# A state-space and attention layer: the pacing of background products beside attention goes from 62.5 to 57.5 of 64

## Chip, cores and metric

One NeuronCore of one Trainium2 chip runs the whole layer. The metric is device time in microseconds (us) of one execution, as the median of three runs. Times in the rows below are us from the start of the profiled span. Engines: PE is TensorE, PEld its weight loads, DVE is VectorE, ACT is ScalarE, POOL is GpSimd, and SP issues the transfers (DMA).

## What is computed

The reference is a decoder layer on x (2048 tokens by 1024 channels, float32). In short:

```python
u    = layer_norm(x) * (1 + scale) + shift
x_ssm, z_ssm, q, k, v, f, z_attn, g_ssm, g_attn = split(u @ w_in)
a, b = split(gelu(s5(x_ssm)) @ w_glu)
y1   = (a * sigmoid(b) * silu(z_ssm)) @ w_proj_ssm
y2   = (forgetting_attention(q, k, v, f) * silu(z_attn)) @ w_proj_attn
out  = layer_norm(alpha * x + ((sigmoid(g_ssm) * y1 + sigmoid(g_attn) * y2) @ w_out) * gate)
```

Attention has 8 heads of 64 channels, is causal, and subtracts a running forgetting bias from the scores.

## The kernel before

**Stages.** Up to about 1010 us the kernel normalizes x, projects it, and runs the state-space scan. Then comes attention, with the products of w_glu and w_proj_ssm beside it (to 1619.5 us). The merge products (w_proj_attn), the output projection (w_out) and the last layer norm close the program. Every float32 product is split into a high and a low part and made of three matmuls.

**Rounds of attention.** One round handles a pair of query blocks (256 queries) of a head: 64 rounds, 8 to a head, numbered 0 to 63 (`rounds`, in `hybrid_layer`). In round p of a head there are 256*(p+1) keys, so the first rounds of a head are short and the last are long. `scores` issues score matmuls (`sc<-ks,qd`), and DVE subtracts the bias and takes maxima (`srow<-sc,fb`). `exponentials` runs on ACT (`srow<-srow,nm`), and DVE writes the reciprocal of the sum (`lb`). `weights_times_v` transposes on PE (`pt<-ident,srow`). Then ACT and DVE copy the result in two parts (`ph`, `pl`), and PE multiplies them by v (`acc<-ph,vs`, `acc<-pl,vs`). The first thing PE writes with a round's `lb` is `acc<-ident,lb`, one per round: it serves below as the mark of a round. `normalize` closes a round on POOL and stores it (`oz_sc<-oo`).

**Products beside it.** `background` has 64 such products: 32 of w_glu and 32 of w_proj_ssm. One product is `mm4`: 12 matmuls into one bank (`bg<-bh,wh`, `bg<-bl,wh`, `bg<-bh,wl`), 512 columns each. Of the last 32, each takes a place of a ring of three (`zt`): SP loads a gate into it (`zt<-gs_sc`), DVE combines it with the product (`zt<-zt,bg`, 128x512), and SP stores the result (`ms_sc<-zt`). After them `background` makes the 64 merge products (12 matmuls of 256 columns each, in banks `bg` and `pt`), which also take places of `zt` (`zt<-ga_sc` and `zt<-ms_sc` fill the halves). ACT and POOL split a result (`mh`, `ml`) for the output projection (`pp<-woh,mh` and so on).

**What sets the order.** The order on every engine is fixed when the program is built. `Model` keeps a rough clock, and `merge` emits from the first stream, in order of rank, whose next step would not wait. `exponentials`, `weights_times_v`, `normalize` and `scores` rank first; then `finish`, `tail`, `inputs`, `weight_chunks` and `background`; `output`, which loads w_out (`wor<-in_w_out_dram`) and splits it (`woh` on ACT, `wol` on DVE and POOL), comes after them. A merge product also waits for `"fin" in done`, and `output` sets that after attention has ended. So `output` is emitted when `background` cannot go on.

**The pacing.** `share(r)` tells how many products must have been emitted before the scores of round r may be, in proportion to the keys up to there:

```python
return AHEAD * (36 * h + p_ * (p_ + 1) / 2) / (36 * NH) - 3
...
yield until(lambda: ck["jobs"] >= share(r))
```

Where the attention streams would wait, `background` is emitted whether or not the share is reached.

Of the kernel before, what the change touches and what calls it, by code (L numbers as in the profile page):

```python
# [16 lines left out]
S = 2048  # L17
D = 1024
NW = 4          # token windows of 512
WT = 512  # L20
KD = D // 128
NG = 32         # state-space groups
GH = 16         # channels of a group
CL = 8          # tokens of a chunk
NCH = S // CL   # chunks
CW = WT // CL   # chunks of a window
NH = 8
# [9 lines left out]
PKN = 163       # of a group: Bbar 16 | swapped 16 | C 16 | swapped 16 | tables 64 | powers 19 | A^7..A^0 16  # L37
# [4 lines left out]
class Model:  # L42
    """A rough clock of the engines, by which the order of emission is chosen (it computes no data)."""

    # from the end of an instruction to the start, on another engine (or the same), of one that needs it
# [34 lines left out]
    def deps(self, e, kw):  # L80
        """When the operands are there for engine e (whose own accesses are in order)."""
        rd, wt = self.aps(kw)
        r = 0.0
        for n in rd:
            if n in self.wr:
                end, by = self.wr[n]
                r = max(r, end + self.lat(e, by))
            for h in self.held:
                if n in h[2]:           # (a transfer that is still to come)
                    r = max(r, max(h[0] + 1100, self.t["sp"] + 1100, self.t["dma"]) + 1700)  # L90
# [43 lines left out]
    def run(self, e, op, kw):  # L134
# [11 lines left out]
        for n in wt:  # L146
            # parts of a tile that transfers fill do not wait for each other
            self.ac.setdefault(n, {})["in" if e == "sp" else e] = end
            self.wr[n] = (end, e)

    def settle(self, rd, wt, dma=False):
        """Emit what is held and has to come before a read of rd and a write of wt (transfers may fill parts of a
        tile in any order)."""
# [14 lines left out]
    def merge(self, streams):  # L168
        """Emit from the first stream whose next step would not wait; streams come in order of rank."""
# [27 lines left out]
class Engine:  # L197
    """An engine whose instructions the model sees."""
# [14 lines left out]
    def when(self, **kw):  # L213
        """When an instruction with these operands could start."""
# [3 lines left out]
    def soon(self, op, /, **kw):  # L218
        """A stream's step: the instruction, emitted once it would not wait."""
# [3 lines left out]
    def later(self, op, /, **kw):  # L223
        """The instruction, emitted once its operands are there (the streams go on meanwhile)."""
# [6 lines left out]
def hybrid_layer(ctx: ExitStack, tc: tile.TileContext, x, c, w_ada, b_ada, w_in, b_f, lam_re, lam_im,  # L231
# [32 lines left out]
    def pround(o, i):  # L264
        """Pool's copy into float32r (its rounding)."""
# [19 lines left out]
    # maskb[q, k] = 0 where k <= q, NEG elsewhere  # L285
# [4 lines left out]
    # ------------------------------------------------------------------ phase 1: input projection  # L290
    esl = ExitStack()               # left: until the projection is done
# [11 lines left out]
    def ps_tile(n=[0]):  # L303
        """One of four banks, which attention later has for scores (three) and outputs."""
# [7 lines left out]
    def bg_tile(n=None):  # L312
        if n is not None and n % 4 > 1:         # (the banks of the transposes, once attention is done)
            return pt_tile()
# [5 lines left out]
    def bank():  # L320
        """Whichever of the two banks of bg_tile is free."""
# [12 lines left out]
    def split_wide(raw, n):  # L334
        """A stream that splits a chunk of weights; the tiles are there at once."""
# [8 lines left out]
    def rstd_of(p, mv, n):  # L344
        """1 / sqrt(var + eps) of the variances mv[:, :, 1]."""
# [21 lines left out]
    def until(f):  # L367
        """A condition to wait on, whatever the time."""
        return lambda: 0.0 if f() else None

    def modulation():
        """shift | 1 + scale of silu(c) @ w_ada + b_ada, as columns, 128 channels at a time."""
# [3 lines left out]
        act.activation(out=one, in_=ident[:, 0:1], func=AF.Sqrt)    # (its table is there when the layer norm needs it)  # L376
# [43 lines left out]
    def early_keys():  # L420
        """Two column tiles of the keys' weights, with which the first window goes on while the next one comes."""
# [7 lines left out]
    def modulation_columns():  # L429
        """Sums over the partitions, as columns."""  # L430
# [17 lines left out]
    def column_sums(acc, n, c0):  # L448
        """mods[:, c0:] = sums of acc over its partitions, as columns, + b_ada."""
# [34 lines left out]
    def normalized():  # L484
        """Windows of tokens, less their mean and over their spread."""
# [21 lines left out]
    def modulated():  # L507
        """u = normalized * (1 + scale) + shift, channels on partitions."""
# [28 lines left out]
    def low_parts():  # L537
        """The two parts of u."""
# [23 lines left out]
    def products_of(ps, w, hi, lo, c0):  # L562
        """A tile of columns of the projection of a window."""
# [7 lines left out]
    def store_parts(kind, m, w, ps):  # L571
        """Queries (scaled) or keys, in two parts."""
# [92 lines left out]
    # the other columns, with the state-space branch alongside  # L665
# [55 lines left out]
    def forget_bias():  # L721
        """f_sc[h, t] = cumulative log_sigmoid(f + b_f)."""
        with ExitStack() as es:
# [10 lines left out]
            # log1p(e) = 2 artanh(s), s = e / (2 + e) <= 1/3  # L734
# [25 lines left out]
    def gate():  # L760
        """The gate part of the modulation, as a row (scaled by 1/16, which the merge leaves)."""
# [17 lines left out]
    def ssm_params():  # L779
        """Per group: input and output matrices, powers and phases, written to pk_sc."""  # L780
        with ExitStack() as es:
            p0 = pl(es, "spp", side="right")
            pk = p0.tile([128, NG, PKN], F32, name="pk")
            uv = p0.tile([128, 4, NG], F32, name="uv")    # phase of A^8 (cos, sin), zoh (re, im)
# [22 lines left out]
            # cosine and sine of arg = n pi/2 + r  # L807
# [21 lines left out]
            od, ev = t32(), t32()       # quadrant: odd * sign, even * sign  # L829
# [7 lines left out]
            def lin(o, p0_, q0, p1, q1, sub):  # L837
                """o = p0 q0 +- p1 q1"""
# [10 lines left out]
            # 0..8: real A^k, both halves; 9..17: imaginary A^k, [-; +]; 18: |A|^8; 19, 20: phase of A^8  # L849
# [941 lines left out]
```

## Time and profile before

| what | value |
|---|---|
| runs, device time | 1916.01, 1917.60, 1920.11 us (median 1917.6) |
| span of the profiled execution, first to last instruction | 1913.3 us |
| median less span (launch and end) | 4.3 us |
| PE busy | 1833.8 us (96%) |
| DVE, ACT, POOL busy | 1082.5 (57%), 775.1 (41%), 923.6 us (48%) |
| attention with its products | about 1012 to 1619.5 us |
| last product to first output matmul | 1623.6 to 1656.7 us |

For the profiled execution the span is what is given of its own time; the runs are timed without the profiler. PE is busy nearly all the time, so the places to look at are those where it is not, and those where its granted clock is below 1.00.

### The profile page before, as it was taken

How to read it: one execution, taken by the hardware profiler on the slowest of the kernel's cores; microseconds unless marked ns; L12 is line 12 of the kernel's file. 1: busy time of each engine (PE TensorE's matmuls, PEld its weight loads, DVE VectorE, ACT ScalarE, POOL GpSimd, SP SyncE). 2: the span in 40 equal slices, each digit the busy share in tenths (PEclk: the TensorE clock that was granted, in tenths of full speed). 3: DMA queues.
4: the chain of work that ended last, by engine and by line, in shares of the span. 5: the costliest groups of instructions: out<-in, count | busy, mean ns of one | idle time of the engine just before them, and what ended most of it. 6: DMA issues, size and time to landing. Idle time of an engine off the chain costs nothing. (4 is left out here: it accounts for less than half of the span.)

```text
span 1913.3 us, 30538 instructions
## 1 busy us (share of the span) xinstructions
PE 1833.8 (96%) x10104; PEld 1565.5 (82%) x10104; DVE 1082.5 (57%) x2886; ACT 775.1 (41%) x1849; POOL 923.6 (48%) x1343
## 2 busy tenths in 40 slices
PE   4999999998999999999998999999999999899997
PEld 3789988886787888888887888988889888788886
DVE  8651114734555555552004777876777866567666
ACT  5441111121433444443114767876767866311110
POOL 5222111113889999995306566376543436533110
PEclk9899999998999999999998999999999999999999
DMA  9434346654333333335217365265364543744432
GB/s 302 138 86 119 94 110 183 149 133 121 101 94 105 100 105 97 105 101 138 91 50 189 98 169 140 77 183 152 113 201 131 151 137 127 260 146 136 131 123 89
DMA packets 276915, 252.37 MB, mean 132 GB/s; under 512 B 66396, under 2 KB 211828, under 8 KB 276756
## 3 DMA queue, kind: packets, MB, share of 16 engines
q1 hardware_dynamic: 276756, 250.41, 45.7%
q8 instruction: 80, 1.31, 0.3%
q14 instruction: 79, 0.65, 0.1%
HBM read 159.50 MB, written 86.63 MB: 129 GB/s over the span
## 5 line engine op out<-in xcount | busy, mean ns | idle before, releaser
L209 PE MATMUL pp<-uh,hi 128*128 128x512 f32 x1136 | 451.0, 397 | 0.0
L209 PE MATMUL pp<-uh,lo 128*128 128x512 f32 x1136 | 446.0, 393 | 0.0
L209 PE MATMUL pp<-ul,hi 128*128 128x512 f32 x1136 | 445.1, 392 | 0.0
L209 ACT ACTIVATE st<-pp 128x512 f32<-128x512 f32 (+2 forms) x168 | 93.9, 559 | 439.1 <-PE pp L209 383.4
L209 DVE TENSOR_TENSOR pl<-pt,ph 128x512 fp32r<-128x512 f32 (+1 forms) x288 | 183.3, 657 | 122.3 <-ACT ph L209 121.7
L209 PEld LDWEIGHTS pp<-uh,lo 128*128 128x128 f32 x1136 | 214.2, 189 | 46.3
L209 PEld LDWEIGHTS pp<-uh,hi 128*128 128x128 f32 x1136 | 216.4, 190 | 41.5
L209 PEld LDWEIGHTS pp<-ul,hi 128*128 128x128 f32 x1136 | 214.7, 189 | 41.9
L209 ACT ACTIVATE srow<-srow,nm 128x512 f32<-128x512 f32 (+2 forms) x320 | 207.6, 653 | 0.4 <-DVE nm L209 0.3
L209 ACT ACTIVATE ph<-pt 128x512 fp32r<-128x512 f32 (+1 forms) x288 | 159.8, 572 | 64.4 <-PE pt L209 51.6
L209 DVE CUSTOM_DVE_ANT_0 srow<-sc,fb 128x512 f32<-128x512 f32 (+3 forms) x288 | 163.0, 594 | 21.9 <-PE sc L209 21.9
L209 PE MATMUL sc<-ks,qd 128*128 128x512 f32 (+2 forms) x640 | 163.7, 381 | 7.1 <-DMA qd<-q_sc 7.1
L209 PE MATMUL pt<-ident,srow 128*128 128x128 f32 x1088 | 159.3, 275 | 8.7 <-DVE pl L209 4.7
L209 PE MATMUL acc<-ph,vs 128*128 128x256 f32 x576 | 163.0, 308 | 2.5 <-POOL ph L209 2.5
L209 POOL TENSOR_TENSOR oo<-oo 64x256 f32<-64x256 f32 x128 | 93.7, 732 | 143.0 <-ACT oo L209 140.0
L209 POOL TENSOR_SCALAR hi<-raw 128x512 fp32r<-128x512 f32 x60 | 39.9, 665 | 237.8 <-PE pp L209 191.7
L209 PEld LDWEIGHTS pt<-ident,srow 128*128 128x128 f32 x1088 | 128.4, 141 | 27.2 <-DVE pl L209 9.5
L209 PE MATMUL acc<-pl,vs 128*128 128x256 f32 x576 | 147.4, 282 | 0.5 <-DVE pl L209 0.5
L209 PE MATMUL bg<-bh,wh 128*128 128x512 f32 (+1 forms) x384 | 140.2, 365 | 5.1 <-DVE zt L209 5.1
L209 PE MATMUL bg<-bh,wl 128*128 128x512 f32 (+1 forms) x384 | 138.1, 360 | 0.0
L209 PE MATMUL bg<-bl,wh 128*128 128x512 f32 (+1 forms) x384 | 137.8, 359 | 0.0
L209 PEld LDWEIGHTS sc<-ks,qd 128*128 128x128 f32 x640 | 107.9, 193 | 24.4 <-issue 8.4
(240 smaller groups left out, 3811.3 us busy)
## 6 DMA issues: line engine op xcount, KB each, us to landing
xt<-in_x_dram SPq DMA_DIRECT2D x32, 512.0 KB, 3.7
qd<-q_sc SPq DMA_DIRECT2D x64, 256.0 KB, 5.4
raw<-in_w_in_dram SPq DMA_DIRECT2D x30, 512.0 KB, 4.5
wada<-in_w_ada_dram SPq DMA_DIRECT2D x16, 512.0 KB, 7.0
k_sc<-st SPq DMA_DIRECT2D x32, 256.0 KB, 3.3
v_sc<-st SPq DMA_DIRECT2D x32, 256.0 KB, 2.3
q_sc<-st SPq DMA_DIRECT2D x16, 512.0 KB, 3.3
gs_sc<-st SPq DMA_DIRECT2D x32, 256.0 KB, 2.3
```

The lines of the kernel that those rows point to most:

```text
L209: return fn(kw["out"], 0.0) if op == "memset" else fn(**kw)
```

## The change

One number: `AHEAD`, the products that the pacing asks for by the end of attention.

```diff
-    AHEAD = 62.5    # products beside attention, of 64, that it has by its end
+    AHEAD = 57.5
```

(The diff also drops comments.) No instruction is added or removed: PE has 10042 matmuls and transposes both ways, 768 of them with 512 columns for the 64 products. What moves is the order. The first 6025 of PE's instructions keep it (to round 21). Of the 768 matmuls, 750 stood ahead of the last `acc<-pl,vs` of round 63 before, and 714 stand there now: 36 matmuls, or three products, have moved behind it. From round 55 to that last matmul PE's order is the same as before.

PE, rounds 35 to 36 (behind the mark of round 35), before:

```order
L209 MATMUL sc<-ks,qd 128x512 x6
L209 MATMUL bg<-bh,wh 128x512
L209 MATMUL bg<-bl,wh 128x512
L209 MATMUL bg<-bh,wl 128x512
L209 MATMUL acc<-ph,vs 128x256
L209 MATMUL acc<-pl,vs 128x256
L209 MATMUL acc<-ph,vs 128x256
L209 MATMUL acc<-pl,vs 128x256
L209 MATMUL bg<-bh,wh 128x512
L209 MATMUL bg<-bl,wh 128x512
L209 MATMUL bg<-bh,wl 128x512
```

and now, from the same score matmuls to the mark of round 36:

```order
L209 MATMUL sc<-ks,qd 128x512 x6
L209 MATMUL acc<-ph,vs 128x256
L209 MATMUL acc<-pl,vs 128x256
L209 MATMUL acc<-ph,vs 128x256
L209 MATMUL acc<-pl,vs 128x256
...
L209 MATMUL pt<-ident,srow 128x128 x8
L209 MATMUL sc<-ks,qd 128x512 x6
L209 MATMUL pt<-ident,srow 128x128 x4
L209 MATMUL sc<-ks,qd 128x256 x2
L209 MATMUL sc<-ks,qd 128x512 x2
L209 MATMUL acc<-ident,lb 128x128
```

Before, 12 product matmuls stood between the marks of rounds 35 and 36; now none does, and four more score matmuls do. Over rounds 35 and 36 together it is 24 before and 9 now, with six more score matmuls; over rounds 27 and 28 it is 15 and 3, with four more.

SP, from the last gate load of the 64 products to the loads of w_out, before:

```order
L209 DMA ms_sc<-zt 128x512
L209 DMA zt<-gs_sc 128x512
L209 DMA ms_sc<-zt 128x512
L209 DMA zt<-ga_sc 128x256
L209 DMA zt<-ms_sc 128x256
L209 DMA ms_sc<-zt 128x512
L209 DMA zt<-ga_sc 128x256
L209 DMA zt<-ms_sc 128x256
L209 DMA oz_sc<-oo 64x256
L209 DMA wor<-in_w_out_dram 128x1024 x3
L209 DMA ms_sc<-zt 128x512
```

and now:

```order
L209 DMA ms_sc<-zt 128x512
L209 DMA zt<-gs_sc 128x512
L209 DMA wraw<-in_w_proj_attn_dram 128x4x128
L209 DMA ms_sc<-zt 128x512
L209 DMA zt<-ga_sc 128x256
L209 DMA zt<-ms_sc 128x256
L209 DMA ms_sc<-zt 128x512
L209 DMA zt<-ga_sc 128x256
L209 DMA zt<-ms_sc 128x256
L209 DMA wor<-in_w_out_dram 128x1024 x3
L209 DMA ms_sc<-zt 128x512
```

The store of the last round (`oz_sc<-oo`) moved ahead by a few issues. The loads of w_out keep their place: behind the store of the last product but one, and ahead of the store of the last.

DVE, behind the second merge product, before:

```order
L209 TENSOR_TENSOR wol_18474<-wor,woh_18472 128x512 x3
L209 SCALAR_TENSOR_TENSOR zt<-zt,pt 128x256
L209 TENSOR_TENSOR zt<-zt 128x256
L209 SCALAR_TENSOR_TENSOR zt<-zt,pt 128x256
L209 TENSOR_TENSOR zt<-zt 128x256
L209 SCALAR_TENSOR_TENSOR zt<-zt,bg 128x256
L209 TENSOR_TENSOR zt<-zt 128x256
L209 TENSOR_TENSOR wol_18474<-wor,woh_18472 128x512 x2
```

and now:

```order
L209 TENSOR_TENSOR wol_18474<-wor,woh_18472 128x512 x2
L209 SCALAR_TENSOR_TENSOR zt<-zt,pt 128x256
L209 TENSOR_TENSOR wol_18474<-wor,woh_18472 128x512
L209 TENSOR_TENSOR zt<-zt 128x256
L209 SCALAR_TENSOR_TENSOR zt<-zt,pt 128x256
L209 TENSOR_TENSOR zt<-zt 128x256
L209 TENSOR_TENSOR wol_18474<-wor,woh_18472 128x512
L209 SCALAR_TENSOR_TENSOR zt<-zt,bg 128x256
```

The third piece of w_out moved one step back, the fourth moved ahead of the fifth merge product. On PE three output matmuls (`pp`) now stand ahead of the 13th merge product and six more ahead of the 14th; before, all 14 came ahead of the first output matmul.

## Rows read from the trace of the kernel before

**Rows 1.** Windows by stage; columns: us, busy us (x instructions) per engine, PEclk, DMA share, GB/s.

```profile
1217.50:1534.80 317.30, 310.40 (x1999) 273.74 (x1998) 244.00 (x793) 231.55 (x586) 162.94 (x261) 0.99 0.50 146
1623.60:1656.70 33.10, 24.16 (x169) 23.29 (x169) 18.99 (x31) 13.15 (x26) 25.02 (x25) 0.90 0.85 277
1656.70:1903.60 246.90, 246.90 (x1370) 215.72 (x1368) 165.95 (x350) 26.24 (x71) 59.61 (x72) 1.00 0.41 132
```

**Rows 2.** Timeline of PE: first product matmul behind attention, first merge product, one at low clock, the ninth.

```profile
1619.53 0.39 PE L209 MATMUL bg<-bh,wh 128*128 128x512 f32 x1
...
1623.64 0.28 PE L209 MATMUL bg<-bh,wh 128*128 128x256 f32 x1
...
1637.09 0.41 PE L209 MATMUL pt<-bh,wh 128*128 128x256 f32 x1
...
1640.75 0.28 PE L209 MATMUL bg<-bh,wh 128*128 128x256 f32 x1
```

**Rows 3.** Timeline of PE: matmuls with idle time before them, in brackets with the releaser.

```profile
1334.83 0.30 PE L209 MATMUL acc<-ident,lb 128*128 128x128 f32 x1 [1.45 <-DVE lb L209]
...
1352.73 0.30 PE L209 MATMUL acc<-ident,lb 128*128 128x128 f32 x1 [0.97 <-DVE lb L209]
...
1636.28 0.58 PE L209 MATMUL pt<-bh,wh 128*128 128x256 f32 x1 [3.86 <-DVE zt L209]
...
1646.13 0.39 PE L209 MATMUL bg<-bh,wh 128*128 128x256 f32 x1 [3.79 <-DVE zt L209]
...
1653.18 0.39 PE L209 MATMUL bg<-bh,wh 128*128 128x256 f32 x1 [0.97 <-DVE zt L209]
...
1655.19 0.39 PE L209 MATMUL bg<-bh,wh 128*128 128x256 f32 x1 [0.32 <-DVE zt L209]
```

**Rows 4.** Windows from round mark to round mark: rounds 27, 28, 33, 34, 35, 36.

```profile
1269.65:1276.79 7.14, 7.14 (x50) 6.43 (x49) 6.44 (x25) 4.44 (x11) 3.34 (x7) 1.00 0.36 100
1276.79:1286.66 9.87, 9.87 (x67) 8.53 (x66) 8.92 (x30) 7.81 (x21) 9.55 (x13) 1.00 0.68 205
...
1326.51:1334.83 8.32, 5.87 (x36) 4.74 (x35) 4.42 (x16) 4.69 (x14) 4.40 (x9) 1.00 0.88 234
1334.83:1342.39 7.56, 7.56 (x40) 6.82 (x41) 5.96 (x23) 4.51 (x11) 5.06 (x7) 0.77 0.53 154
1342.39:1352.73 10.34, 9.37 (x58) 7.97 (x57) 8.62 (x27) 8.07 (x23) 10.05 (x14) 1.00 0.45 123
1352.73:1361.94 9.21, 9.21 (x62) 8.32 (x63) 8.95 (x29) 6.32 (x15) 4.67 (x8) 1.00 0.63 192
```

**Rows 5.** The page's costliest groups: DVE's operation on a score tile.

```profile
L209 DVE CUSTOM_DVE_ANT_0 srow<-sc,fb 128x512 f32<-128x512 f32 (+3 forms) x288 | 163.0, 594 | 21.9 <-PE sc L209 21.9
```

**Rows 6.** Timeline of SP's queue behind attention.

```profile
1621.48 0.32 SPq L209 DMA_DIRECT2D zt<-ga_sc  x1
...
1622.38 0.38 SPq L209 DMA_DIRECT2D ms_sc<-zt  x1
1625.13 0.32 SPq L209 DMA_DIRECT2D zt<-ga_sc  x1
...
1626.02 0.47 SPq L209 DMA_DIRECT2D oz_sc<-oo  x1
1626.58 1.50 SPq L209 DMA_DIRECT2D wor<-in_w_out_dram  x3
```

**Rows 7.** Timeline of DVE behind attention.

```profile
1623.84 0.69 DVE L209 SCALAR_TENSOR_TENSOR zt<-zt,bg 128x512 f32<-128x512 f32 x1 [2.03 <-PE bg L209]
...
1634.67 1.22 DVE L209 TENSOR_TENSOR wol<-wor,woh 128x512 fp32r<-128x512 f32 x1 [0.46 <-ACT woh L209]
1635.82 0.41 DVE L209 SCALAR_TENSOR_TENSOR zt<-zt,pt 128x256 f32<-128x256 f32 x1
...
1638.38 0.41 DVE L209 SCALAR_TENSOR_TENSOR zt<-zt,bg 128x256 f32<-128x256 f32 x1
...
1640.98 0.69 DVE L209 TENSOR_TENSOR wol<-wor,woh 128x512 fp32r<-128x512 f32 x1 [1.11 <-ACT woh L209]
```

## The prediction

> **What bounds the kernel now.** I first read the windows by stage, to see where PE is not full. In the output projection it is: 246.90 of 246.90 us busy at a granted clock of 1.00 [rows 1]. In the stretch of attention in which the order changes (rounds 21 to 54) it is busy 310.40 of 317.30 us, so 6.9 us are idle. Between the last of the 64 products and the first output matmul it is busy only 24.16 of 33.10 us, at a granted clock of 0.90 [rows 1]. So attention is close to PE-bound, and the hole behind it is the worst place: 8.94 us idle, and about (1 - 0.90) x 33.1 = 3.3 us of clock.
>
> Next I looked at each gap. The hole has four: 3.86, 3.79, 0.97 and 0.32 us, 8.94 in all, and each ends with DVE's work on a `zt` tile [rows 3]: a merge product cannot start because its bank has not been emptied. A matmul of 256 columns lasts 0.41 us behind the first gap against 0.28 before it [rows 2], the half clock of 1.2 GHz. In attention the idle time is made of gaps of about 1 us, and the two shown end with DVE's `lb` [rows 3]: there the softmax chain was late.
>
> Last, I read DVE and SP in the hole. DVE's operation for the third merge product starts at 1635.82, behind a `wol` that waited for ACT [rows 7], and that in turn for w_out. The loads of w_out start at 1626.58 [rows 6], 2.9 us after the last product ended on PE at 1623.64 [rows 2].
>
> **The change, part by part.** PE's work is the same; 36 matmuls move. From 1619.53 to 1623.64 PE made 18 of them [rows 2]: 4.11 / 18 = 0.228 us each, so 36 take 8.2 us.
>
> 1. *Attention, rounds 21 to 54: -8.2 us*, if PE stays as full as it was.
> 2. *Behind attention: +8.2 us.* The three products run there back to back, at full clock. What they issue must keep pace: a load into `zt`, 0.69 us on DVE [rows 7] and a store. The store at 1622.38 let the next load of that place go at 1625.13 [rows 6], so it took 2.75 us. Taking a load of as many bytes at the same, a place is held about 6.2 us, and three places give a product every 2.1 us; PE needs 12 x 0.228 = 2.7 us. So SP's extra pairs of transfers and DVE's operations are hidden, by some 0.6 us a product; without that cover PE would wait for them.
> 3. *DVE in the thinned rounds: +1.4 us.* Rounds 35 and 36 lose 15 product matmuls and gain six score matmuls, that is three tiles. PE was busy 9.37 + 9.21 = 18.58 us there [rows 4]; it now needs 18.58 - 15 x 0.228 + 6 x 0.228 = 16.5 us (score matmuls taken at the price of others with up to 512 columns). DVE was busy 8.62 + 8.95 = 17.57 us [rows 4]. With three more tiles of 0.594 us [rows 5] and one combination of 0.69 us less it needs 18.7 us, 2.2 more than PE. Rounds 27 and 28 lose 15 - 3 = 12 and gain four. PE: 17.01 - 2.7 + 0.9 = 15.2 us. DVE: 6.44 + 8.92 + 1.2 - 0.69 = 15.9 us, 0.7 more. Upper end: 2.9 us, if DVE is filled without a gap and PE waits for all of it. Lower end: nothing, if the neighbouring rounds take up DVE's lag; three score banks and three `ph`/`pl` pairs let it lag a little. I take the middle, since round 35 shows the wait already (0.97 us on `lb`) and rounds 27 and 28 show none [rows 3, 4].
> 4. *The hole: no gain from more cover.* This is the choice on which the forecast rests. One would expect three more products, 8.2 us of PE, to hide the loads of w_out. But the order puts these loads in SP's queue behind the store of the last product but one, before and now alike, and that store comes only when PE has made that product. So w_out still starts about 2.5 to 3 us after the last product, however many products ran before it, and the three that moved pass ahead of it. The store of the last round now stands earlier in SP's queue, which takes one issue of 0.47 us [rows 6] out of the way. I count nothing for that.
> 5. *DVE's order in the hole: 0.* The third merge product no longer waits for the third `wol`: its operation could start at 1634.67 in place of 1635.82 [rows 7], -1.15 us. But the fifth, at 1638.38, now stands behind the `wol` that ran at 1640.98 for 0.69 us [rows 7]. That would let the ninth product, which takes its bank, start at about 1641.9 in place of 1640.75 [rows 2], +1.1 us. I take the middle of the two.
> 6. *Output matmuls ahead of the 13th and 14th merge products: -1.3 us.* Nine of them (9 x 0.228 = 2.1 us) stand where PE idled 0.97 and 0.32 us [rows 3]. Lower bound of this gain: nothing, if their own pieces of w_out are late.
>
> Sum: -8.2 + 8.2 + 1.4 + 0 + 0 - 1.3 = +0.1 us on a span of 1913.3, so 1913.4. The median of the runs lies 4.3 us above this span and I carry that over: **1917.7 us**. The launch, the projection, the scan, rounds 0 to 20 and the last layer norm keep their times.
>
> **The rivals.**
>
> *Filled hole (faster).* The hole goes: 8.94 us of gaps and 3.3 us of clock, with item 3 kept: 1917.6 + 1.4 - 12.2 = 1906.8 us. For it: the gaps are real and the 8.2 us lie right in front of them. Against it: the place of w_out in SP's queue, item 4.
>
> *A lucky head start (faster).* In round 33 PE was busy 5.87 of 8.32 us, 2.45 idle, and through round 34 the granted clock was 0.77, which is 0.23 x 7.56 = 1.7 us [rows 4]. Rounds 33 and 34 are reordered, with 12 product matmuls behind the first scores of round 34. If that wait goes: 1917.7 - 4.2 = 1913.5 us. Against it: the wait began with a late chain, and order alone need not cure it.
>
> *Attention loses its filler (slower).* DVE becomes the bound of rounds 27, 28, 35 and 36 and PE waits for it all, 2.9 us. Each of the two waits lowers the clock as the one in round 33 did, 1.7 us each: 1917.6 + 2.9 + 3.4 - 1.3 = 1922.6 us. [...] For it: PE's 16.5 against DVE's 18.7 us. Against it: 0.7 us in rounds 27 and 28 is small.
> The Trainium skill, Perfetto Trace Analysis, section Optimization Strategy, says that where the most contended engine changes over time, interleaving the regimes may help, which speaks against taking products out of the mixture. By it alone none of the 8.2 us would come back in attention, and the sum would be 1917.6 + 8.2 = 1925.8 us. The trace bears that out only for the rounds of item 3: over all changed rounds PE is at 98% and DVE at 77% (310.40 and 244.00 of 317.30 us [rows 1]).
>
> *Nothing moves.* This falls out: the order shows three products behind attention that were beside it, not five, since the kernel emits products as filler whatever the pacing says.
>
> **How the numbers follow.** A measurement of this kernel can tell about 0.2%, 3.8 us: faster is below 1913.8, slower above 1921.4. I give the forecast 0.48, with a range of its own of 1914 to 1921 (item 3 from 0 to 2.9, item 5 from -1.15 to 1.1, item 6 from -1.3 to 0, and a gap of an attention round more or less). The filled hole has 0.13, the lucky head start 0.14, the lost filler 0.25. Faster: 0.13, 0.09 of the head start, which lies near the line, and 0.05 from the lower edge of the forecast, 0.27. Slower: the lost filler, and 0.02 of the upper edge, 0.27. Within 0.2%: 0.46. The range for 8 in 10 is 1911 to 1924: it takes in the forecast, the head start and the lost filler with a little beyond it, and leaves out the filled hole.
>
> **What would show it.** Right: attention's last matmul about 7 us earlier than 1619.5; the last product about 1 us later than 1623.64; w_out issued 2.5 to 3 us after that product; two gaps of 3 to 4 us in the hole again, and the two small ones gone. Item 3 is right if rounds 35 and 36 show 1 to 2 us of PE idle that end with DVE. Wrong: gaps in the hole of less than 4 us together, which would be the filled hole, or a granted clock below 0.9 in rounds 27 to 37, which would be the lost filler.

## The result, and the profile after

The changed kernel takes 1932.56 us (median of 4 runs, 1926.98 to 1934.15), beside 1918.86 for the kernel before on the same chip. The ratio of the runs is 1.0061, 95% interval 1.0043 to 1.0079: slower by 0.6% (11.7 us by this ratio, 13.7 by the two medians), where I forecast no change. Its profiled span is 1930.6 us. That execution lies at the median of its runs, while the profiled one of before (1913.3) was a quick one of its own, so the two profiles differ by 17.3 us and the runs by about 12 to 14. (Its run took 1932.45 us, 1.85 us more than its span. Most of the 4.3 us that stood as launch and end ahead of the prediction was therefore the quick profile of before. The profiles count 10104 matmuls and transposes on PE in either kernel, and the first 6088 come in the same order.) Here is the span cut at the marks of rounds (the `acc<-ident,lb` of each in the timeline of PE); the third column is a second profile of the same kernel, from the experiments.

| us | before | after | after, again |
|---|---|---|---|
| start to mark of round 0 | 1018.8 | 1021.0 | 1019.8 |
| marks 0 to 21 (order unchanged) | 198.7 | 202.4 | 200.5 |
| marks 21 to 55 (36 matmuls fewer) | 317.3 | 313.4 | 313.4 |
| marks 55 to 63 (order unchanged) | 76.7 | 77.0 | 77.6 |
| mark 63 to the end (36 matmuls more) | 301.8 | 316.9 | 315.5 |

Up to round 21 the two kernels have PE's same order; most of the differences there come in the stretches that end with marks 2, 3, 10, 19 and 20, and they vary between profiles of one kernel. I don't explain them. What repeats are the rows with changed order: 8.2 us were to go, and 3.9 went; 8.2 were to come, and 13.7 to 15.1 came. Together that is 9.8 to 11.2 us more, beside the 11.7 and 10.4 us of the two series' ratios.

The 3.9 us are in part chance. Three of the experiments below (e1_hold, g4_q58_before, h2_tail_before) keep the order of before on every engine up to mark 55. They take 314.9, 316.7 and 315.5 us from mark 21 to 55, where this profile of before has 317.3. g2_tail_act keeps the order of after there and takes 314.4. By the means some 2.4 us came back.

The windows of after that answer to [rows 1] (us, then busy us and instructions of PE, PEld, DVE, ACT and POOL, granted clock, DMA share, GB/s):

```profile
1223.38:1536.74 313.36, 303.52 (x1963) 266.76 (x1962) 237.25 (x790) 231.31 (x586) 162.60 (x261) 0.99 0.51 143
...
1621.90:1634.20 12.30, 12.30 (x55) 9.87 (x53) 2.21 (x4) 0.97 (x2) 5.92 (x7) 1.00 0.43 141
1634.20:1673.00 38.80, 25.51 (x158) 23.89 (x158) 18.39 (x28) 12.56 (x25) 27.22 (x26) 0.82 0.78 247
...
1673.00:1920.90 247.90, 247.90 (x1381) 216.87 (x1380) 168.15 (x354) 26.84 (x72) 61.58 (x73) 1.00 0.42 134
```

PE's idle time in the changed stretch of attention rose from 6.90 to 313.36 - 303.52 = 9.84 us. The 54 product matmuls behind attention ran without a gap in 12.30 us, 8.2 more than the 18 before. But the hole behind them grew from 33.10 to 38.80 us, with 13.29 us idle in place of 8.94 and a granted clock of 0.82 in place of 0.90, a mean of its two levels, 1.2 and 2.4 GHz. Its gaps, in PE's timeline (in brackets the idle time and the releaser), where [rows 3] had four:

```profile
1621.81 0.39 PE L209 MATMUL bg<-bh,wh 128*128 128x512 f32 x1
...
1633.87 0.39 PE L209 MATMUL bg<-bh,wl 128*128 128x512 f32 x1
1634.80 0.39 PE L209 MATMUL bg<-bh,wh 128*128 128x256 f32 x1 [0.54 <-DVE zt L209]
...
1639.62 0.39 PE L209 MATMUL bg<-bh,wh 128*128 128x256 f32 x1 [3.14 <-DVE zt L209]
...
1653.58 0.58 PE L209 MATMUL pt<-bh,wh 128*128 128x256 f32 x1 [5.00 <-DVE zt L209]
...
1659.99 0.39 PE L209 MATMUL bg<-bh,wh 128*128 128x256 f32 x1 [1.62 <-DVE zt L209]
...
1663.94 0.39 PE L209 MATMUL bg<-bh,wh 128*128 128x256 f32 x1 [2.24 <-DVE zt L209]
...
1668.99 0.39 PE L209 MATMUL pt<-bh,wh 128*128 128x256 f32 x1 [0.36 <-DVE zt L209]
...
1671.77 0.39 PE L209 MATMUL bg<-bh,wh 128*128 128x256 f32 x1 [0.39 <-DVE zt L209]
```

Each still ends with DVE's work on a `zt` tile. What DVE waited for is in its timeline, and it is not PE:

```profile
1634.06 0.69 DVE L209 SCALAR_TENSOR_TENSOR zt<-zt,bg 128x512 f32<-128x512 f32 x1 [4.51 <-DMA zt<-gs_sc]
...
1638.88 0.69 DVE L209 SCALAR_TENSOR_TENSOR zt<-zt,bg 128x512 f32<-128x512 f32 x1 [4.14 <-DMA zt<-gs_sc]
...
1642.65 0.42 DVE L209 SCALAR_TENSOR_TENSOR zt<-zt,bg 128x256 f32<-128x256 f32 x1 [3.08 <-DMA zt<-ga_sc]
```

And this is SP's queue there, which answers to [rows 6]:

```profile
1621.59 0.32 SPq L209 DMA_DIRECT2D ms_sc<-zt  x1
1623.88 0.32 SPq L209 DMA_DIRECT2D zt<-gs_sc  x1
1624.31 0.38 SPq L209 DMA_DIRECT2D wraw<-in_w_proj_attn_dram  x1
1624.74 0.50 SPq L209 DMA_DIRECT2D ms_sc<-zt  x1
1631.21 0.32 SPq L209 DMA_DIRECT2D zt<-gs_sc  x1
...
1632.18 0.54 SPq L209 DMA_DIRECT2D ms_sc<-zt  x1
1634.93 0.32 SPq L209 DMA_DIRECT2D zt<-gs_sc  x1
1635.30 0.43 SPq L209 DMA_DIRECT2D wraw<-in_w_proj_attn_dram  x1
1635.82 0.46 SPq L209 DMA_DIRECT2D ms_sc<-zt  x1
1640.15 0.32 SPq L209 DMA_DIRECT2D zt<-ga_sc  x1
...
1641.04 0.38 SPq L209 DMA_DIRECT2D ms_sc<-zt  x1
1643.79 0.32 SPq L209 DMA_DIRECT2D zt<-ga_sc  x1
...
1644.68 1.33 SPq L209 DMA_DIRECT2D wor<-in_w_out_dram  x3
```

Store and load alternate. A load into a `zt` place waits until the store from that place has landed (2.3 to 6.5 us from issue to issue), and the next store stands behind it in the queue, though its data may be long there. So SP made a pair in about 4.9 us ((1641.04 - 1621.59) / 4), where PE makes a product in 2.74. The pairs differ: the two stores that went out right behind a load of weights (`wraw`) held up the next load for 6.5 and 4.3 us, and their pairs took 7.4 and 5.2 us; the other two pairs took 3.2 and 3.6 us. w_out followed at 1644.68, 10.6 us after the last product's end near 1634.1; before it was 2.9.

In attention I compared the stretches between marks one by one. How many matmuls each gained or lost is from the order of PE, priced at the 0.228 us of the prediction; "left" is what that does not explain.

| marks | matmuls, product and score | priced | before | after | left |
|---|---|---|---|---|---|
| 25 to 26 | -3, -2 | -1.1 | 8.54 | 9.74 | +2.3 |
| 27 to 29 | -12, +4 | -1.8 | 17.01 | 16.61 | +1.4 |
| 33 to 35 | +12, +4 | +3.6 | 15.88 | 16.61 | -2.9 |
| 35 to 37 | -15, +6 | -2.1 | 19.55 | 18.02 | +0.5 |
| 43 to 44 | none | 0 | 10.09 | 8.50 | -1.6 |
| 49 to 50 | none | 0 | 8.32 | 12.48 | +4.2 |
| the other 25 | -18, -12 | -6.8 | 237.9 | 231.4 | +0.4 |
| 21 to 55 | -36, 0 | -8.2 | 317.3 | 313.4 | +4.3 |

(In the experiments, round N is the stretch that ends with mark N, so that round 50 runs from mark 49 to 50, and rounds 26 to 28 from mark 25 to 28; in [rows 4] and in the prediction it is the one that begins with mark N.) Two places lose most. The window of before from mark 25 to 26, those of after from mark 25 to 28, and the gap that ends the first of these, in PE's timeline:

```profile
1254.14:1262.68 8.54, 8.21 (x46) 6.30 (x45) 7.54 (x32) 6.12 (x17) 7.26 (x12) 1.00 0.72 178
```

```profile
1260.13:1269.87 9.74, 7.66 (x42) 5.46 (x40) 9.52 (x31) 7.11 (x19) 9.36 (x13) 1.00 0.71 183
1269.87:1278.46 8.59, 8.59 (x51) 7.57 (x52) 4.76 (x20) 3.73 (x10) 4.22 (x6) 1.00 0.62 204
1278.46:1287.24 8.78, 7.95 (x51) 6.34 (x49) 8.06 (x30) 7.45 (x21) 5.10 (x9) 1.00 0.49 132
```

```profile
1269.87 0.33 PE L209 MATMUL acc<-ident,lb 128*128 128x128 f32 x1 [2.02 <-DVE lb L209]
```

From mark 25 to 26 DVE is now busy 9.52 of 9.74 us, and PE waits 2.02 us for `lb`; in the order, six product matmuls that stood right ahead of this mark have moved behind it. The third window answers to the first of [rows 4]: there PE now idles 8.78 - 7.95 = 0.83 us, DVE is busy 8.06.

The other place is marks 49 to 50. The windows, before and after:

```profile
1478.34:1486.66 8.32, 8.32 (x49) 7.11 (x48) 8.11 (x35) 5.90 (x16) 6.20 (x10) 1.00 0.88 243
```

```profile
1477.04:1489.52 12.48, 10.17 (x49) 8.40 (x48) 9.26 (x40) 6.00 (x16) 5.27 (x9) 0.86 1.01 278
```

PE has the same 49 instructions in both. Before, it is never idle; now it idles 2.31 us, and the granted clock is 0.86, between its two levels, which is 0.14 x 12.48 = 1.7 us. The two make up nearly all of the 4.2 us.

### The profile page after: what moved, and what is told of

Read it like the earlier page. It is cut to its first block, busy times and chain, and to the rows that moved or that the text cites. A ratio compares the mean times of both kernels' runs of the same rounds, so it can differ in the third digit from the quotient of the medians.

```text
span 1930.6 us, 30554 instructions
## 1 busy us (share of the span) xinstructions
PE 1838.5 (95%) x10104; PEld 1566.7 (81%) x10104; DVE 1079.0 (56%) x2886; ACT 774.7 (40%) x1849; POOL 927.5 (48%) x1343
```

## Experiments

Ratios are to the kernel before, timed on the same chip, with 95% intervals. "Tail" is mark 63 to the end; before it is 301.8 us, in after 316.9. Several edits need a second name for a queue: `spx = Engine(M, "sp", nc.scalar)` (or `nc.gpsimd`) issues from ACT's (POOL's) queue; PE and DVE keep their order in all of these.

**a1_again.** No edit: the changed kernel once more.

> The changed kernel once more, for a second profile of it. First profile against the one of before: from the mark of round 0 to that of round 63 attention took 592.8 us against 592.6, so none of the 8.2 us of the moved matmuls came back, and from the mark of round 63 to the end 316.9 us against 301.8. Theory 1 (SP's order at the head starts: the store of a round's output stands behind more loads, ACT waits for a free output buffer): the wait before round 50 comes again with 2 us or more, because the order there differs from before; the wait before round 19, where the order is the same as before, was chance and may be gone. Theory 2 (chance alone made attention long): both are gone and attention takes about 584 us. About 1.005 to 1.008 of before in either case.

Measured: 1929.75 us, ratio 1.0054 [1.0035, 1.0073]. The slowdown repeats, and with it 313.4 us for marks 21 to 55 and a tail of 315.5.

**e1_hold.** The pacing of before, but the last four products are held back until attention has ended:

```diff
-                yield until(lambda: 8 + m in ck["tiles"])
+                yield until(lambda: 8 + m in ck["tiles"] and (w < NW - 1 or m < 4 or done.get("tt", 0) == len(rounds)))
```

> Pacing of before, but the last four products are held until attention's last matmul is emitted: 48 product matmuls stand behind attention in place of 18, and no round before 60 is changed. Theory 3 (behind attention the ring of three zt places cannot keep up with products made back to back, since SP issues each load only after the store ahead of it has landed): the tail from the mark of round 63 grows by the 6.8 us of the 30 matmuls and 5 to 7 us more, and the whole is 5 to 7 us slower than before (1.003 to 1.004). Rival (the tail in the changed kernel was long for another reason, the order of w_out among the merge products): the same time as before within 2 us.

Measured: ratio 1.0008 [0.9999, 1.0018], tail 306.6 us. Behind mark 63 stand 48 product matmuls, 21 more than the 27 before (in after it is 63), and 21 x 0.228 is the 4.8 us by which the tail grew: here the work behind attention cost its matmuls and nothing else. The 5 to 7 us that theory 3 asked of this run did not come. In SP's timeline one gate load alone stands behind attention's last matmul (1618.62), since the held products had their places loaded earlier:

```profile
1622.94 0.54 SPq L209 DMA_DIRECT2D ms_sc<-zt  x1
1625.34 0.33 SPq L209 DMA_DIRECT2D zt<-gs_sc  x1
...
1633.96 1.37 SPq L209 DMA_DIRECT2D wor<-in_w_out_dram  x3
```

The last product ended near 1629.7, so w_out came 4.3 us after it and not 10.6. So more products behind attention need not cost extra; in after three of their gate loads ran through SP's queue there, and here one. That is not the only difference: no load of weights stands there in this run either, and two do in after.

**e2_mid.** The low pacing up to round 43, the old one from round 44:

```diff
-            return AHEAD * (36 * h + p_ * (p_ + 1) / 2) / (36 * NH) - 3
+            return (AHEAD if r < 44 else 62.5) * (36 * h + p_ * (p_ + 1) / 2) / (36 * NH) - 3
```

> Pacing 57.5 up to round 43 and 62.5 from round 44: the rounds up to 43 are thinned as in the changed kernel, then attention catches up, and 27 product matmuls stand behind attention in place of 18 before and 54 changed. If theory 1 or lost filler in rounds 24 to 43 made attention long, it is 3 to 6 us slower than before. If the cost lies behind attention (theory 3) and in rounds 44 to 55, it is within 2.5 us of before.

Measured: ratio 1.0013 [1.0003, 1.0024], tail 304.0 (27 product matmuls behind). Marks 25 to 28 take 27.1 us (22.65 before, 27.11 in after) and marks 49 to 50 take 13.0, as in after; marks 57 to 58 take 9.1, where before has 13.4. So both losses come with the low pacing ahead of them, and the tail's with the pacing at the end.

**e3_ms_act** and **g2_tail_act.** The changed kernel with all stores `ms_sc<-zt` (e3), or only the last six (g2), on ACT's queue, so that no load stands behind a store's wait (g2's edit; e3's has `spx` alone):

```diff
-            sp.later("dma_start", out=ms_sc[...], in_=zt)
+            (spx if w == NW - 1 and m > 1 else sp).later("dma_start", out=ms_sc[...], in_=zt)
```

> The changed kernel with the stores of the w_proj_ssm products (ms_sc) issued from ACT's queue; no order of instructions on PE, DVE, POOL changes, and SP keeps its order without these stores. Theory 3: the stores no longer stand in SP's queue behind loads that wait, so the products behind attention keep pace with PE, w_out is issued about 3 us after the last product in place of 10.5, and the time falls by 5 to 8 us from the changed kernel, to 1.002 to 1.004 of before. Rival (the ring itself is too small or the transfers too slow): within 2 us of the changed kernel.

> The changed kernel with only the last six stores of the w_proj_ssm products on ACT's queue, where ACT has little left to do; attention keeps its queues. Theory 3 (behind attention each product's store waits in SP's queue behind a load that waits for the landing of the store before): the time from the mark of round 63 to the end falls from 316 to 310 or 311 us and attention stays at 592 us, so the whole is about 5 us faster than the changed kernel. Rival: the tail stays above 314 us.

Measured: e3 1.0152 [1.0135, 1.0169], tail 311.1, but attention 20 us longer, since ACT now waits for what the stores wait for: 32.4 us in 13 waits that end with DVE's `zt`, where after has none. g2 1.0046 [1.0031, 1.0061], tail 311.9: of 6.9 us of excess (316.9 - 301.8 - 8.2) 5.0 are gone. (The ratio's interval overlaps that of after; the tail is what tells.) g2's queues in the timeline of SP and ACT:

```profile
1632.17 0.32 SPq L209 DMA_DIRECT2D zt<-gs_sc  x1
...
1633.58 0.32 SPq L209 DMA_DIRECT2D zt<-gs_sc  x1
...
1636.69 0.32 SPq L209 DMA_DIRECT2D zt<-ga_sc  x1
...
1640.67 1.37 SPq L209 DMA_DIRECT2D wor<-in_w_out_dram  x3
```

Two gate loads now follow at 1.4 us. The last product ends near 1637.0, and w_out follows 3.6 us behind it. The loads of weights stand in SP's queue here too (1627.31 and 1633.95). That SP's alternation of stores and loads makes most of the excess is shown by this run; the same edit brings nothing in the kernel before (h2_tail_before). The other 2 us stay open.
The Trainium skill, DMA: Bandwidth & Descriptors, section Issuing engines are not separate DMA queues, says that transfers of several engines share the same 16 DMA engines and that issuing from several saves only the time of the issue. By that the six issues would be worth some 2 to 3 us, an estimate (6 x 0.32 to 0.54 us, SP's rows of after). This case differs: 5.0 us came back, because waits stood in the queue between the issues.

**f3_wraw_pool.** The changed kernel with the weight loads `wraw` on POOL's queue, against the thought that they hold up the chain:

```diff
-                sp.later("dma_start", out=raw, in_=src[0]...)
+                spx.later("dma_start", out=raw, in_=src[0]...)
```

> The changed kernel with the loads of weight chunks (wraw) issued from POOL's queue. Theory 4 (behind attention three of these loads stand in SP's queue between the stores of the products, the store right behind one of them lands after 4 to 6 us in place of 2.7, and the next load into the ring waits for it): the time from the mark of round 63 to the end falls from 316 to about 310 or 311 us. Rival (SP is blocked by the stores' own landings, one after the other): it stays above 314 us.

Measured: ratio 1.0086 [1.0057, 1.0115], tail 316.0. Which queue issues the weight loads makes no difference to the tail. This does not clear the loads themselves: POOL issued one at 1620.47, SP the store at 1620.93, and the next load went out at 1626.89, again 6.0 us behind the store. In after, its repeat, this run and h1_oz48 the eight product stores ahead of w_out's loads that went out within 0.6 us behind a weight load held up the next load for 4.3 to 6.5 us, the others for 2.2 to 3.3. No run takes the weight loads alone away from there.

**g3_early.** The low pacing up to round 28 only (`AHEAD if r < 29 else 62.5` in the line of e2_mid), so that 18 product matmuls follow attention as before:

> Pacing 57.5 up to round 28 and 62.5 from round 29: rounds 22 to 28 are thinned as in the changed kernel, from round 31 on the counts are those of before, and 18 matmuls stand behind attention as before. Theory 5 (the thinned rounds lose filler where PE then waits for DVE and ACT): rounds 26 to 28 take 27 us in place of 22.7, later rounds and the tail are as before, and the whole is 3 to 5 us slower than before. Rival (what is lost there is won back in the next rounds): within 1.5 us of before.

Measured: ratio 1.0032 [1.0021, 1.0042], tail 301.9. Marks 25 to 28 take 10.03 + 10.04 + 8.76 = 28.8 us (22.65 before), with 24 product matmuls as before and after; marks 49 to 50 are at 8.32 again. PE's timeline at mark 26, and the windows from mark 25 to 27:

```profile
1270.50 0.48 PE L209 MATMUL acc<-ident,lb 128*128 128x128 f32 x1 [2.34 <-DVE lb L209]
```

```profile
1260.47:1270.50 10.03, 7.65 (x41) 5.46 (x39) 9.81 (x31) 7.10 (x19) 9.65 (x14) 0.99 0.73 189
1270.50:1280.54 10.04, 10.04 (x52) 8.93 (x53) 5.94 (x20) 3.77 (x10) 4.62 (x6) 0.84 0.47 163
```

With the early rounds alone at the low pacing the kernel is slower by 6 us (0.32% of 1919): the lost filler stands by itself. The rounds behind win little of it back: from mark 21 to 31, with 117 product matmuls in both, this run takes 98.4 us where before took 93.5. Behind the wait of 2.34 us the granted clock was 0.84 up to mark 27, a mean of the two levels, 1.2 and 2.4 GHz.

**f4_ahead66.** `AHEAD = 66.5`, the other direction: no product matmul behind attention.

> The other way: pacing 66.5, by which no product is left behind attention (18 matmuls before). If products behind attention cost their own 0.228 us a matmul and nothing else, as in the held kernel, the tail from the mark of round 63 falls by about 6 us (27 matmuls) from 301.8 us, and attention grows by as much where PE is full: the same as before within 3 us. If thinned rounds are what made the changed kernel slow, filler added to rounds 27 to 43 makes those rounds no shorter but takes away the waits, and the whole is 2 to 4 us faster than before.

Measured: ratio 1.0073 [1.0053, 1.0093], tail 294.4, attention (marks 0 to 63) 17 us longer. Both expectations miss. The 27 matmuls more in attention are 6.2 of the 17 us; nearly all the rest is waiting, for PE is idle 34.9 us there and 24.5 in before. More filler early costs too.

**Round 50 (marks 49 to 50).** ACT's copy `oo<-acc` of round 49 waits for the landing of a store of `oo` (two buffers), and PE behind it. The rows of after, ACT, PE and SP:

```profile
1481.57 1.00 ACT L209 ACTIVATE oo<-acc 64x384 f32<-64x384 f32 x2 [5.15 <-DMA oz_sc<-oo]
```

```profile
1483.32 1.76 PE L209 MATMUL pt<-ident,srow 128*128 128x128 f32 x7 [2.31 <-ACT srow L209]
```

```profile
1469.48 0.32 SPq L209 DMA_DIRECT2D ms_sc<-zt  x1
1471.65 0.32 SPq L209 DMA_DIRECT2D zt<-gs_sc  x1
1472.02 0.45 SPq L209 DMA_DIRECT2D za<-za_sc  x1
1472.56 1.25 SPq L209 DMA_DIRECT2D qd<-q_sc  x2
...
1475.50 0.48 SPq L209 DMA_DIRECT2D oz_sc<-oo  x1
```

SP stood still ahead of 1469.48 for a product's data and then 2.2 us for its landing. The round's loads went out 10.4 us after mark 47 (1461.61); in before it was 6.1 (1469.00 against 1462.90). The store at 1475.50 landed only about 6 us later. Six runs looked for the row that decides.

**f1_oz_pool** and **f2_oz_pool_before.** All stores `oz_sc<-oo` on POOL's queue, in the changed kernel and in the one before:

```diff
-            sp.later("dma_start", out=oz_sc[...], in_=v)
+            spx.later("dma_start", out=oz_sc[...], in_=v)
```

> The changed kernel with the store of each round's output (oz_sc) issued from POOL's queue, right behind the POOL operation that makes it; SP keeps its order without these stores. Theory 1 (at head starts the store waits in SP's queue behind loads of keys and queries, so ACT waits for its output buffer): round 50 falls from 12.5 us to 8 to 9 us, round 58 from 14.4 to 11 or less, rounds 18 to 20 lose their scatter, and the whole is 5 to 10 us faster than the changed kernel. Rival (the wait is the transfer time of the key loads, whatever queue the store is in): rounds 50 and 58 stay within 1 us.

> The kernel before with the same store on POOL's queue. Theory 1: round 58 falls from 13.4 us to 11 or less, rounds 10, 19 and 34 by 1 us or so, and the whole is 4 to 8 us faster than before. Rival: within 2 us of before, or slower if issuing from POOL costs POOL's time (64 stores).

Measured: f1 1.0065 [1.0044, 1.0085]. Rounds 50 and 58 fall to 8.31 us each, but round 10 rises to 17.99, round 18 to 10.28 and round 59 to 9.24, and the sum is no better. f2 1.0051 [1.0035, 1.0066]: round 58 falls to 8.37, rounds 10 and 18 rise in the same way.

**g1_q50** and **g4_q58_before.** The loads of queries at round 50 (changed kernel) or round 58 (kernel before) are put off by a round:

```diff
-            if at["qr"] < min(r + 3, len(rounds)) and ...
+            if r != 50 and at["qr"] < min(r + 3, len(rounds)) and ...
```

> The changed kernel; the load of queries that the scores of round 50 trigger waits for the next round, so that it and the key loads no longer all stand ahead of the store of round 48 in SP's queue. PE's order keeps its counts. Theory 1: round 50 falls from 12.5 to 8 to 9 us, nothing else moves, and the whole is about 4 us faster than the changed kernel. Rival: the wait moves on (round 51 or 52 grows) and the whole stays within 1.5 us.

> The kernel before; the load of queries that the scores of round 58 trigger waits for the next round. Theory 1 says that the same queue costs the kernel before its longest wait in attention: round 58 falls from 13.4 to 9 to 10 us and the whole is 3 to 4 us faster than before. Rival: the wait is the transfers themselves, and round 58 and 59 together stay at 19.5 us.

Measured: g1 1.0061 [1.0044, 1.0078], round 50 at 13.84; g4 1.0001 [0.9988, 1.0014], round 58 at 13.77. Both miss: these loads are not the cause.

**h1_oz48.** Round 48's store alone on POOL's queue (`spx if (h, p_) == (6, 0) else sp`):

> The changed kernel with a single store moved: that of round 48's result goes through POOL's queue, all others stay on SP. PE, DVE and ACT keep their order. Theory (the store of round 48 stands too late in SP's queue, behind the loads that wait, so that ACT lacks its oo buffer): round 50 falls from 13.8 to between 8.3 and 9.7 us, rounds 58 and 59 and the tail stay as in the changed kernel (13.8, 8.4 and 315 to 317 us); ratio to before 1.003 to 1.0045. Rival (what is late at round 50 is a load, not this store): round 50 stays at 13.5 to 14 us, ratio 1.005 to 1.0065.

Measured: ratio 1.0069 [1.0054, 1.0084], round 50 at 12.99. The theory falls: ACT waits for the store ahead of it, round 47's. (After has 12.48 there, not the 13.8 that the expectation starts from.)

**i1_pair48.** The product's store at 1469.48 and the gate load behind it on POOL's queue, nothing else:

```diff
-            sp.later("dma_start", out=ms_sc[...], in_=zt)
+            (spx if (w, m) == (1, 2) else sp).later("dma_start", out=ms_sc[...], in_=zt)
...
-            sp.later("dma_start", out=zt, in_=...)
+            (spx if (kind, w, m) == ("h", 1, 5) else sp).later("dma_start", out=zt, in_=...)
```

> The changed kernel with one pair of transfers moved: the store of the 11th state-space result and the gate load behind it, at the marks of rounds 47 and 48, go through POOL's queue; nothing else moves. Theory: at round 50 SP is late because it waits 3.5 us for that store's data and 2.2 us for its landing, so the loads of the coming rounds and the store of a finished round go out in one crowd, at a DMA share of 1.0 to 1.2. Without the pair SP issues these loads some 5 us earlier against mark 47, and round 50 falls from 12.5 to 13 us to between 8.3 and 10 us; other rounds and the tail stay; ratio to before 1.0035 to 1.005. Rival (the crowd comes whenever these loads are issued, or the wait passes on to POOL): round 50 stays at 12 us or more, ratio 1.0055 to 1.007.

Measured: ratio 1.0054 [1.0038, 1.007]. Round 50 falls to 8.32 us as the theory has it, and round 49 rises from 4.49 to 10.45 as the rival has it: the wait for the landing passed on to POOL, which makes `ph`'s and `fd`'s parts for the next round. POOL's timeline:

```profile
1468.10 0.75 POOL L209 DMA_DIRECT2D ms_sc<-zt  x1 [2.05 <-DMA qd<-q_sc]
1474.74 0.56 POOL L209 DMA_DIRECT2D zt<-gs_sc  x1 [5.89 <-DMA ms_sc<-zt]
```

So the pair that holds up SP is what made round 50 long, by way of the store of round 47 behind it: with either of the two out of SP's queue (this run, f1) round 50 is 8.3 us. In this run POOL, which issued the pair, paid for the landing.

**h2_tail_before** and **h3_both_cures.** The last six product stores on ACT's queue in the kernel before (h2); in the changed kernel this and h1's edit (h3):

> The kernel before, pacing 62.5, with the last six stores of products through ACT's queue in place of SP's. If SP's chain of loads and stores is short enough before (18 matmuls behind attention, w_out issued 2.9 us after the last product), nothing is to be had: tail 301 to 303 us, ratio 0.999 to 1.001. Rival (the chain costs in the kernel before too): the tail falls to 297 to 300 us, ratio 0.997 to 0.9985, which would beat both kernels.

> The changed kernel with both cures: round 48's store on POOL's queue, the last six stores of products on ACT's. If the two costs are separate and add, round 50 is 8.3 to 9.7 us and the tail 311 to 312.5 us, ratio to before 1.001 to 1.0025; what is left over the kernel before is then rounds 26 to 28 (some 4.5 us) and the rest of the tail (some 2 us), less what rounds 31 to 38 gain. Rival (one cure gives back the other, as in the runs in which all these stores were moved): ratio 1.004 or more.

Measured: h2 1.0015 [1.0004, 1.0027], tail 302.9 and round 63 longer by 1.7 us: nothing to be had in the kernel before. h3 1.0028 [1.0018, 1.0039], tail 310.7, round 50 at 10.56. The tail's cure holds a second time; as h1's edit alone left round 50 at 12.99, I don't count the rest of h3 as its effect. No version tried beats the kernel before; e1_hold and g4_q58_before come level with it.

## Why the prediction was wrong

**Item 1 (attention -8.2 us, "if PE stays as full as it was") failed by 4.3 us, 1.4 of which item 3 had.** 3.9 us came back (2.4 by the means above). The two losses that no step had are the wait at mark 26 (2.3 us) and marks 49 to 50 (4.2 us, 1.7 of them clock), where the order of PE did not change at all: there SP was held up by a product's store and load that now stand elsewhere in its queue. I had gone through PE's and DVE's orders in attention and not through SP's. The wait at mark 26 is the rival of the lost filler, at a place that it had not named, and g3_early shows it alone. Its price for the clock, 1.7 us a wait, was not paid there in after, where the granted clock stayed at 1.00 behind 2.02 us; it was paid at marks 49 to 50 (0.86 behind 2.31 us), for another reason, and in g3_early (0.84 behind 2.34 us).
The rule of the Trainium skill that the prediction weighed (Perfetto Trace Analysis, Optimization Strategy: interleave regimes that lean on different engines) is borne out by about half: by it alone nothing would come back in attention, and 3.9 of 8.2 us did.

**Item 2 (behind attention +8.2 us, SP hidden "by some 0.6 us a product") failed by 5.5 to 6.9 us.** The products themselves took their 8.2 us; what SP was late came out in the hole behind them. This is the largest error and a step of the working: I divided the time for which a place is held by three places. The places do overlap; SP's queue does not. Behind attention the stores and loads alternate in it, each load waits for the store right ahead, and a pair took 4.9 us against PE's 2.74. e1_hold (one gate load and no weight load in the queue there, no excess), g2_tail_act and h3_both_cures (stores out of the queue, some 5 us back) show it. [Rows 6] already had 2.75 us from store to load, 0.32 us for the issue of that load and the next store behind it, so a pair of at least 3.07, more than PE's 2.74, could be read there. That two stores would hold up a load for 6.5 and 4.3 us could not; but the weight load ahead of one of these two stands in SP's new order ahead of the prediction, and I passed over it.

**Item 3 (+1.4 us in the thinned rounds, 0 to 2.9)** came out in size, and partly by luck: marks 27 to 29 and 35 to 37 left 1.4 + 0.5 = 1.9 us. PE idles 0.83 us in each pair, where before had none and 0.97, so only 0.7 us of the 1.9 is new waiting. The rest is PE's own busy time, 15.78 and 17.19 us against the 15.2 and 16.5 of the sum. I had the larger share in the second pair; it was in the first.

**The lucky head start** of marks 33 to 35 (4.2 us in the prediction) came for the most part: 2.9 us. The 2.45 us of idle time were two waits, 1.01 and 1.45 us, and both are gone. The clock's 1.7 us were partly chance: with the order of before, e1_hold and h2_tail_before waited 2.6 and 2.5 us there and kept a clock of 1.00, while g4_q58_before fell to 0.78. Another 1.6 us came at marks 43 to 44, where PE's order is the same: a wait of 1.41 us ahead of mark 44, which stands in before and in its three repeats, is gone. Why is open. The two kept attention from coming out longer than before.

**Item 4 (no gain in the hole; w_out 2.5 to 3 us after the last product)** was right in that the hole was not filled, and right that the stores order w_out. The distance was 10.6 us, a consequence of item 2, and the hole grew by 5.7 us (4.35 of them idle, the rest busy time at the lower clock).

**Items 5 and 6** (0 and -1.3 us) drown in that: the hole's gaps are other gaps now. The two small ones did not vanish; seven stand where four were.

By the prediction's own signs: attention's last matmul came at 1621.69 and not 7 us earlier than 1619.5 (5.9 us of that had been lost ahead of mark 21); the last product ended 10.5 us later than 1623.64, not one; and gaps of 3.14 and 5.00 us stand in the hole again. Rounds 35 and 36 show 0.83 us of idle time, not 1 to 2. The clock stayed at 1.00 in rounds 27 to 37, so the sign of the lost filler did not come, though filler was lost ahead of mark 26.

## What to carry to other kernels

Where one queue issues, in order, both the store that frees a place of a ring and the load that refills it, see whether each load stands right behind the store that it waits for. Here it did, and a ring of three places made one pair per landing: compare that time, not the place's divided by the ring, with what the engine needs. Work taken out of a mixed stretch is not got back at its busy time: read, round by round, which wait the removed instructions stood in front of. Moving such a wait to another engine's queue helped where that engine had little left to do (g2_tail_act, h3_both_cures), and cost more than it gave where it had (e3_ms_act, i1_pair48).

## What the runs showed that I had not expected

The store issued at 1624.74 let its place go only 6.47 us later, and for much of that time almost nothing else moved. Windows of half a microsecond (the last two columns are the DMA share and GB/s):

```profile
1628.50:1629.00 0.50, 0.50 (x4) 0.42 (x3) 0.14 (x1) 0.00 (x0) 0.00 (x0) 1.00 0.06 12
1629.00:1629.50 0.50, 0.50 (x4) 0.42 (x3) 0.50 (x1) 0.00 (x0) 0.00 (x0) 1.00 0.08 10
1629.50:1630.00 0.50, 0.50 (x3) 0.40 (x3) 0.04 (x1) 0.00 (x0) 0.00 (x0) 1.00 0.07 18
```

A share of 0.06 to 0.08 is what one of the 16 DMA engines gives when it alone is busy (1/16 = 0.0625): the transfer seems to wait for one straggler. What it moved can be told from the sizes of the packets in these 1.5 us:

```profile
DMA packets 37, 0.02 MB, mean 14 GB/s; under 512 B 3, under 2 KB 35, under 8 KB 37
```

All but 5 of the 37 have 512 B or more and less than 2 KB. A row of a `wraw` tile is 128 float32, 512 B; a row of the store is 2 KB. Of the transfers under way only the weight load issued at 1624.31 has such rows. So that load was late, and the store issued right behind it landed after it. Why one engine lagged is open; an instruction load ran on one of them just before (from 1627.5 to 1628.0 queue q8 has one packet and 11.9% of 16 engines, 0.95 us), but the profile doesn't say on which. I had also not expected how well rounds repeat: the stretches that end with marks 36 to 41 and 51 to 57 agree within 0.05 us between after and its repeat (35, 42 and 58 within 0.6 us), so that a single profile of a variant can tell such a round's change of a microsecond from chance. That does not hold for every round: marks 34 to 35 take 7.56, 6.00, 7.47 and 6.01 us in before and its three repeats.
